# A hybrid decoder block on one core: where the state-space tables are made, and when their rest runs

## The chip, the core and the metric

The kernel runs on one of the eight cores of a Trainium2 chip. Time is device time of one execution in microseconds (us), from the start of the program to its end. The kernel before has a median of 2892.49 us in three runs (2890.32 to 2893.48). Its profiled execution, from which all rows come, took 2894.66 us, with a span of 2892.9 us from the first to the last instruction.

A core has five engines with a queue of instructions each: TensorE (PE, matmuls; its weight loads are listed as PEld), VectorE (DVE), ScalarE (ACT), GpSimd (POOL) and SyncE (SP). Each works through its own queue in order; they wait for each other by semaphores. Here SP issues the loads of weights, and nearly all other transfers are issued by POOL, in the order in which they stand in its queue. A transfer whose issue waits holds up all that stand behind it in that queue.

## The reference

One decoder block on 512 tokens with 16 learned meta tokens ahead (528 rows, width 2048), all in float32. Attention with low-rank queries and keys (MLA) and a diagonal complex state-space layer (S5) run in parallel on the same normalised input:

```python
n = rms_norm(h, norm_mix)
q_lat, kv_lat, k_r, u, gates = split(n @ w_in)          # widths 512, 512, 64, 1024, 4096
q, kv = rms_norm(q_lat) @ w_q_up, rms_norm(kv_lat) @ w_kv_up
attn_out = softmax(causal(q k^T)) v @ w_attn_proj       # 16 heads, rope on 64 dims
y = gelu(s5_scan(u, ...))                               # 64 groups of 16 inputs, 64 states
ssm_out = (y @ w_glu_val) * sigmoid(y @ w_glu_gate)
h += (sigmoid(g0) * attn_out + sigmoid(g1) * ssm_out) @ w_out
h += (silu(m @ w_ffn_gate) * (m @ w_ffn_up)) @ w_ffn_down   # m = rms_norm(h)
out = rms_norm(h)[:, 16:]
```

The scan is x_t = a x_(t-1) + B u_t with y_t = Re(C x_t) + D u_t, where a, B and C follow from parameters by exponentials, sines and complex products. What depends on the parameters alone is called tables here.

## The kernel before

**Matmuls.** A float32 weight tile is split into a high part (`whi`, a rounded copy made by ACT) and a rest (`wlo`, a subtraction on DVE); so is each moving operand. A product is the sum of three matmuls. `dense` (L389) makes a tile of 128 output columns from weight blocks of 128 x 1024: eight slices by three products, 24 matmuls of 512 columns, or 48 of 264 where all 528 rows are made. Such a run over one weight block is called a block below. `Weights.use` (L280) splits the block that comes two later (`AHEAD`), so a split stands in the queues of ACT and DVE between the work of neighbouring blocks.

**Work beside the blocks.** After each block `bg()` (L363) runs first the calls in `later` that are due, then each generator given to `beside`, up to an allowance: a `yield` names the cost of what was just issued in units of about a microsecond, and the generator goes on while its account is positive. So the order of instructions is that in which this code is written out.

**First stage (0 to 305 us).** Tiles j = 0 to 7 of `u` over 16 blocks; `rstd` of the input comes in tile 2, and `evac_u` (L864) empties the first three tiles then. After these, four tiles of the query latent (8 blocks), four of the key latent (8 blocks) and one of the rope key (2 blocks). `ssm_first` (L730) runs beside them from tile 1 on with an allowance of 4.0: `ssm_params` (L518), then for each of four groups of states `ssm_tables` (L665: the rotation table `ER`, an expansion in two halves into `ssA`, its products on PE into `psQ`, and its transposes on PE into `psB`, kept as `bd`) and, for the first three groups, `ssm_powers` (L717: another expansion, kept as `cd`). `normed` (L891) turns the key latent into operands in four pieces (rows `ev<-H`, `H<-ev` on DVE). `run_out()` (L929) issues what is left of the generator behind the last block, and only then come the load of the rope table `in_kcs`, the rotation of the rope key, and the attention's first products (`up_rope`).

**Attention (305 to 584 us).** Heads are pipelined by hand; the change does not touch it.

**Attention projection (584 to 850 us).** 16 tiles of two blocks each, 32 blocks, `ev` buffers for the results and stores to `ao`. Beside them run `ssm_main` (L737, one step per block) and `x_products` (L1353), which loads x in eight pairs, scales them on DVE and stores them with three combinations to `xd`, operands of the gates. `ssm_main` first loads `U`, `ER` and the output tables, makes the power table of the last group, and loads `ssA` from `bd`. Then each group takes five steps: `states` of the first half (PE, from `ssA` and `U`) with `rotate` (DVE) and the second `outputs` of the group before; `states` of the second half, then the loads of `ssA` and `U` for the next group, the stores of results (`yd`) and the loads of the output tables (`ssB` from `kd`, eight transfers, and two of `cd`); `scan`; `back`, and the load of `ER` for the next group, which has a single buffer; and the first `outputs`. From tile 12 on the gates' operands are loaded and split (L1374).

**After 850 us** follow the gates, the gated unit, the output projection and the feed-forward layer. The change does not touch them.

Of the kernel before, what the change touches and what calls it, by code (L numbers as in the profile page):

```python
# [297 lines left out]
def _emit(nc, sp, pp, dp, A, out):  # L298
# [45 lines left out]
    ed = dp.tile([4, P, 4 * BP * NC_], F32, name="ed")  # L344
# [3 lines left out]
    c3 = dp.tile([P, 2 * BP * 48], F32, name="c3")  # L348
# [316 lines left out]
    def ssm_tables(b):  # L665
# [14 lines left out]
        ER = sb([P, 4, BP, NC_], F32, "ER")  # L680
        for i in range(2):
            ACT.activation(ER[:, 2 * i, :, :18], tabs["rt"][i][:, js], AF.Copy)
        POOL.memset(ER[:, 3, :, 0], 0.0)
        DVE.tensor_copy(ER[:, 3, :, 1:], e8[:, 2, js].unsqueeze(2).to_broadcast([P, BP, NC_ - 1]))
        yield 0.7
        for m, k in ((17, 17), (34, 31)):
            double((ER[:, 0], ER[:, 2]), m, k, BP, T1, T2)
            yield 1.0 + 0.05 * k
        ts(ER[:, 1], ER[:, 2], -1.0, None, MUL)
        POOL.dma_start(ed[b], ER.rearrange("p a j c -> p (a j c)"))  # L690
        yield 0.5
# [22 lines left out]
        if b == 3:  # L714
            POOL.dma_start(c3, C48.rearrange("p a j q -> p (a j q)"))

# [13 lines left out]
    def ssm_first():  # L730
        yield from ssm_params()
        for b in range(4):
            yield from ssm_tables(b)
            if b < 3:
                yield from ssm_powers(b)

    def ssm_main():  # L737
# [16 lines left out]
        def load_e(b):  # L754
            ER = sb([P, 4, BP * NC_], F32, "ER")
            POOL.dma_start(ER.rearrange("p a n -> p (a n)"), ed[b])
            nxt_["E", b] = ER

# [66 lines left out]

        load_u(0)
        load_e(0)
        load_t(0)
        C48 = sb([P, 2, BP, 48], F32, "sC")
        POOL.dma_start(C48.rearrange("p a j q -> p (a j q)"), c3)  # L830
        tabs["C48"] = C48
        yield 1
        for _ in ssm_powers(3):
            yield 1
        load_b(0)
        nxt_["m"] = [sb([P, 2, T], F32, t) for t in ("T1", "T2", "v", "w")]
        for b in range(4):
            states(b, 0)
            rotate(b, 0)
            if b:  # L840
                outputs(b - 1, 1)
            yield 1
            states(b, 1)
            rotate(b, 1)
            if b < 3:
                load_b(b + 1)
                load_u(b + 1)
            if b:
                store(b - 1)
                load_t(b)  # L850
            yield 1
            scan(b)
            yield 1
            back(b)
            if b < 3:
                load_e(b + 1)
            yield 1
            outputs(b, 0)
            yield 1
        outputs(3, 1)  # L860
# [15 lines left out]
    for j in range(8):  # L876
        if j == 2:
            d2 = ps([P, 2, 512], "D")
            o = [(d2[:, 0, :HT], 0, HT), (d2[:, 1, :HT], HT, T)]
        else:  # L880
            o = halves("A", "B")
        dense(n, KT, o)
        pend.append((j, o))
        if j >= 2:
            while pend:
                evac_u(*pend.pop(0))
        if j == 1:
            beside(ssm_first(), 4.0)
# [464 lines left out]
    def x_products():  # L1353
# [6 lines left out]

        load(0)
        yield 2
        for i in range(8):
            if i < 7:
                load(i + 1)
            for m in range(2):
# [7 lines left out]
    begin = {12: [L("XD", *range(4)), L("XA", *range(4))],  # L1374
             13: [S("XD", *range(4)), L("XA", *range(4, 8)), L("B12", 2)],
             14: [S("XA", *range(4)), L("B12", 3, 0, 1)],
             15: [S("XA", *range(4, 8)), S("B12", *range(4)), L("T12", *range(8))]}
    beside(ssm_main(), 1.0)
    beside(x_products(), 2.2)
    for j in range(KT):  # L1380
        p = ps([P, 512], "A")
        dense(at, KT, [(p, 0, SEQ)])
        t = ev(SEQ)
# [3 lines left out]
        for h in begin.get(j, ()):  # L1387
            h()
# [422 lines left out]
```

## Time and profile before

| | |
|---|---|
| median of 3 runs | 2892.49 us |
| profiled execution | 2894.66 us (span 2892.9 us) |
| PE busy | 2759.4 us, 95% of the span |
| DVE busy | 2049.5 us, 71% |
| ACT busy | 1217.5 us, 42% |
| POOL busy | 478.7 us, 17% |
| PE's share of the chain that ended last | 86% |
| mean granted clock of PE | 0.976 |

The page sums up the whole span, and most of it is one full stage after another; what a change in one stage is worth is read from that stage. So the rows further down are from stretches: how long PE was busy in one, at what granted clock (1.00 is 2.4 GHz, 0.5 is 1.2 GHz), and what it waited for. The time before an instruction in which its engine did nothing stands in brackets at the end of its row, with the engine, tile or transfer that ended it.

### The profile page before, as it was taken

How to read it: one execution, taken by the hardware profiler on the slowest of the kernel's cores; microseconds unless marked ns; L12 is line 12 of the kernel's file. 1: busy time of each engine (PE TensorE's matmuls, PEld its weight loads, DVE VectorE, ACT ScalarE, POOL GpSimd, SP SyncE). 2: the span in 40 equal slices, each digit the busy share in tenths (PEclk: the TensorE clock that was granted, in tenths of full speed). 3: DMA queues.
4: the chain of work that ended last, by engine and by line, in shares of the span. 5: the costliest groups of instructions: out<-in, count | busy, mean ns of one | idle time of the engine just before them, and what ended most of it. 6: DMA issues, size and time to landing. Idle time of an engine off the chain costs nothing.

```text
span 2892.9 us, 50212 instructions
## 1 busy us (share of the span) xinstructions
PE 2759.4 (95%) x20782; PEld 2603.3 (90%) x20782; DVE 2049.5 (71%) x2690; ACT 1217.5 (42%) x1766; POOL 478.7 (17%) x731
## 2 busy tenths in 40 slices
PE   8995999968899999999999999999999999999997
PEld 7984899946779999888889999999999999999997
DVE  7775666655437777543368888888888888878896
ACT  4232555522235444432234444444444445353445
POOL 2032211134430000111213000000000003030102
PEclk9996999989999999999999999999999999999999
DMA  4453222268673443544443333433434336474542
GB/s 169 140 166 117 79 65 66 61 202 282 191 262 128 154 146 132 167 138 146 142 138 115 139 132 132 146 129 123 144 125 139 136 128 248 163 269 153 198 166 96
DMA packets 126788, 431.49 MB, mean 149 GB/s; under 512 B 18240, under 2 KB 23040, under 8 KB 124448
## 3 DMA queue, kind: packets, MB, share of 16 engines
q1 hardware_dynamic: 76672, 263.36, 26.8%
q0 software_dynamic: 49104, 163.82, 17.2%
q8 instruction: 163, 2.67, 0.4%
q10 hardware_dynamic: 784, 1.11, 0.1%
q14 instruction: 65, 0.53, 0.1%
HBM read 344.87 MB, written 77.66 MB: 146 GB/s over the span
## 4 chain that ended last, share of the span: by engine, by line
PE 86%; DVE 6%; DMA 3%; issue 2%; ACT 1%; POOL 1%; DVEq 0%; SPq 0%; ACTq 0%; POOLq 0%
PE psA L316 50%; PE psB L316 22%; PE psQ L316 6%; PE psV L316 5%; PE psD L316 2%; DVE wlo L263 1%; DVE T L323 1%; DVE ev L323 1%; DVE S L323 1%; DMA H<-in_xT 1%; DMA ssA<-bd 0%; PE psB L710 0%; POOL ssB L766 0%; PE psA L1123 0%; ACT whi L262 0%
## 5 line engine op out<-in xcount | busy, mean ns | idle before, releaser
L316 PE MATMUL psA<-S,whi 128*128 128x256 f32 (+2 forms) x5136 | 1124.3, 309 | 20.8 <-DVE ev L323 6.7
L316 PEld LDWEIGHTS psA<-S,whi 128*128 128x128 f32 x5136 | 845.4, 190 | 76.5 <-issue 10.2
L316 PE MATMUL psA<-S,wlo 128*128 128x256 f32 (+2 forms) x2568 | 791.5, 308 | 7.9 <-DVE wlo L263 7.9
L263 DVE TENSOR_TENSOR wlo<-raw,whi 128x1024 fp32r<-128x1024 f32 (+1 forms) x479 | 590.6, 1234 | 190.2 <-ACT whi L262 188.3
L262 ACT ACTIVATE whi<-raw 128x1024 fp32r<-128x1024 f32 (+1 forms) x479 | 504.4, 1055 | 458.1 <-PE psA L316 213.4
L316 PEld LDWEIGHTS psA<-S,wlo 128*128 128x128 f32 x2568 | 485.8, 189 | 34.0 <-DVE wlo L263 8.3
L263 DVE TENSOR_TENSOR wlo<-cmb,whi 128x1024 fp32r<-128x1024 f32 x225 | 274.8, 1221 | 96.4 <-ACT whi L262 95.3
L316 PE MATMUL psB<-S,whi 128*128 128x256 f32 (+1 forms) x1632 | 330.3, 284 | 0.5 <-ACT ssB L711 0.5
L262 ACT ACTIVATE whi<-cmb 128x1024 fp32r<-128x1024 f32 x225 | 237.7, 1056 | 201.5 <-DVE wlo L263 121.6
L316 PEld LDWEIGHTS psB<-S,whi 128*128 128x128 f32 x1632 | 266.2, 190 | 1.3 <-ACT ssB L711 1.0
L316 PE MATMUL psB<-S,wlo 128*128 128x256 f32 (+1 forms) x816 | 230.8, 283 | 0.0
L316 PEld LDWEIGHTS psB<-S,wlo 128*128 128x128 f32 x816 | 154.7, 190 | 0.0
L1331 POOL DMA_DIRECT2D td<-sC x22 | 15.8, 718 | 764.6 <-ACT ev L1250 718.3
L316 PE MATMUL psA<-H,whi 128*128 128x512 f32 (+2 forms) x448 | 120.4, 355 | 8.9 <-DVE ev L323 8.0
L316 PEld LDWEIGHTS psA<-H,whi 128*128 128x128 f32 x448 | 78.2, 192 | 19.9 <-DVE ev L323 8.2
L243 DVE TENSOR_TENSOR cmb<-raw,raw 128x1024 f32<-128x1024 f32 x75 | 91.3, 1218 | 6.3 <-DMA raw<-in_wst 5.2
L323 DVE TENSOR_TENSOR H<-H,psA 128x256 f32<-128x256 f32 (+1 forms) x42 | 22.5, 535 | 97.2 <-POOL H L323 88.2
L243 DVE TENSOR_TENSOR cmb<-cmb,raw 128x1024 f32<-128x1024 f32 x75 | 91.3, 1218 | 0.0
L243 DVE TENSOR_TENSOR raw<-raw,raw 128x1024 f32<-128x1024 f32 x75 | 91.3, 1218 | 0.0
L243 DVE TENSOR_TENSOR cmb<-raw,cmb 128x1024 f32<-128x1024 f32 x75 | 91.3, 1217 | 0.0
L1250 ACT ACTIVATE ev<-psA 128x256 f32<-128x256 f32 x114 | 43.4, 381 | 100.7 <-PE psA L316 100.7
L316 PE MATMUL psA<-H,wlo 128*128 128x512 f32 (+2 forms) x224 | 78.0, 348 | 0.0
(678 smaller groups left out, 5463.4 us busy)
## 6 DMA issues: line engine op xcount, KB each, us to landing
raw<-in_wst SPq DMA_DIRECT2D x485, 512.0 KB, 3.6
td<-sC POOLq DMA_DIRECT2D x22, 512.0 KB, 3.2
td<-H POOLq DMA_DIRECT2D x40, 256.0 KB, 3.3
S<-td POOLq DMA_DIRECT2D x40, 256.0 KB, 6.8
H<-sg POOLq DMA_DIRECT2D x16, 512.0 KB, 4.0
ed<-ER POOLq DMA_DIRECT2D x4, 1056.0 KB, 5.1
ER<-ed POOLq DMA_DIRECT2D x4, 1056.0 KB, 7.8
bd<-ssB POOLq DMA_DIRECT2D x4, 1024.0 KB, 5.2
```

Source lines behind the costliest of these rows:

```text
L243: self.nc.vector.tensor_tensor(t, g(a), g(b), op=op)
L262: self.nc.scalar.activation(hi[:, a:b], w[:, a:b], AF.Copy)
L263: self.nc.vector.tensor_tensor(lo[:, a:b], w[:, a:b], hi[:, a:b], op=ALU.subtract)
L316: PE.matmul(o, lhsT=l, rhs=r, start=start, stop=stop, skip_group_check=more)
L323: eng.tensor_tensor(o, a, b, op=op)
L1250: ACT.activation(snap[name], o, AF.Copy)
L1331: POOL.dma_start(dst[0:2].rearrange("f p n -> p f n"), pair)
```

## The change

Four things change. `ssm_first` makes the power tables of all four groups, starts after tile 2 with an allowance of 5.0, and leaves two of the four parts of `ER` (a sign change and a decay) to be made in the projection, on ACT (`more_e`). `ssm_main` has new steps: loads first, `states` two blocks later, tables and results behind `scan`, `U` of the next group behind `back`, both `outputs` of a group in the two steps of the next. `x_products` begins its loads two and its products three blocks later. The results of the projection go through one buffer (`sC`) in place of three, and the operands of the gates are loaded and split in blocks 26 to 32, in another order.

```diff
-    ed = dp.tile([4, P, 4 * BP * NC_], F32, name="ed")
+    ed = dp.tile([4, P, 2, BP * NC_], F32, name="ed")
...
-        ER = sb([P, 4, BP, NC_], F32, "ER")
+        ER = sb([P, 2, BP, NC_], F32, "ER")
         for i in range(2):
-            ACT.activation(ER[:, 2 * i, :, :18], tabs["rt"][i][:, js], AF.Copy)
-        POOL.memset(ER[:, 3, :, 0], 0.0)
-        DVE.tensor_copy(ER[:, 3, :, 1:], e8[:, 2, js].unsqueeze(2).to_broadcast([P, BP, NC_ - 1]))
-        yield 0.7
+            ACT.activation(ER[:, i, :, :18], tabs["rt"][i][:, js], AF.Copy)
+        yield 0.3
...
-        ts(ER[:, 1], ER[:, 2], -1.0, None, MUL)
...
             yield from ssm_tables(b)
-            if b < 3:
-                yield from ssm_powers(b)
+            yield from ssm_powers(b)
...
-            POOL.dma_start(ER.rearrange("p a n -> p (a n)"), ed[b])
+            POOL.dma_start(ER[:, 0::2], ed[b])
             nxt_["E", b] = ER
+
+        def more_e(b):
+
+            js, ER = slice(b * BP, (b + 1) * BP), nxt_["E", b]
+            d = ER[:, 3].rearrange("p (j c) -> p j c", c=NC_)
+            POOL.memset(d[:, :, 0], 0.0)
+            ACT.activation(d[:, :, 1:], e8[:, 2, js].unsqueeze(2).to_broadcast([P, BP, NC_ - 1]), AF.Copy)
+            ACT.activation(ER[:, 1], ER[:, 2], AF.Copy, scale=-1.0)
...
+        load_b(0)
         load_u(0)
         load_e(0)
-        load_t(0)
-        C48 = sb([P, 2, BP, 48], F32, "sC")
-        POOL.dma_start(C48.rearrange("p a j q -> p (a j q)"), c3)
-        tabs["C48"] = C48
+        nxt_["m"] = [sb([P, 2, T], F32, t) for t in ("T1", "T2", "v", "w")]
         yield 1
-        for _ in ssm_powers(3):
-            yield 1
-        load_b(0)
-        nxt_["m"] = [sb([P, 2, T], F32, t) for t in ("T1", "T2", "v", "w")]
+        yield 1
+        more_e(0)
         for b in range(4):
+            if b:
+                outputs(b - 1, 0)
             states(b, 0)
             rotate(b, 0)
+            yield 1
             if b:
                 outputs(b - 1, 1)
-            yield 1
             states(b, 1)
             rotate(b, 1)
             if b < 3:
                 load_b(b + 1)
-                load_u(b + 1)
+            yield 1
+            scan(b)
             if b:
                 store(b - 1)
-                load_t(b)
-            yield 1
-            scan(b)
+            load_t(b)
             yield 1
             back(b)
             if b < 3:
                 load_e(b + 1)
+                load_u(b + 1)
             yield 1
-            outputs(b, 0)
+            if b < 3:
+                more_e(b + 1)
             yield 1
+        outputs(3, 0)
+        yield 1
         outputs(3, 1)
         store(3)
...
-        if j == 1:
-            beside(ssm_first(), 4.0)
+        if j == 2:
+            beside(ssm_first(), 5.0)
...
+        yield 2.2
+        yield 2.2
         load(0)
-        yield 2
+        yield 2.2
+        load(1)
+        yield 2.2
         for i in range(8):
-            if i < 7:
+            if 0 < i < 7:
                 load(i + 1)
...
-    begin = {12: [L("XD", *range(4)), L("XA", *range(4))],
-             13: [S("XD", *range(4)), L("XA", *range(4, 8)), L("B12", 2)],
-             14: [S("XA", *range(4)), L("B12", 3, 0, 1)],
-             15: [S("XA", *range(4, 8)), S("B12", *range(4)), L("T12", *range(8))]}
+
+    begin = {26: [L("XD", *range(4)), L("B12", 2, 3)], 27: [L("B12", 0, 1), L("XA", *range(4))],
+             28: [S("XD", *range(4)), S("B12", 2)], 29: [S("B12", 3), L("XA", *range(4, 8))], 30: [S("B12", 0, 1)],
+             31: [S("XA", *range(4))], 32: [L("T12", *range(8)), S("XA", *range(4, 8))]}
+    for i, fs in begin.items():
+        later.extend([i, f] for f in fs)
...
-        t = ev(SEQ)
+        t = sb([P, SEQ], F32, "sC")
         ACT.activation(t, p, AF.Copy)
         POOL.dma_start(ao[j], t)
```

Where this puts instructions is seen in the built programs. First DVE at the end of the first stage. In the kernel before the four latent pieces are over when these rows begin: the end of the fourth `ER`, the two halves of its expansion (`T`, `ssA`), `sK` from the products on PE, then the eviction of the rope key (`S<-psA`, `S<-psB`) and its product with the rope table.

```order
L323 TENSOR_TENSOR ER_2562<-T_183_2557,T_184_2558 128x8x31
L330 TENSOR_SCALAR ER_2562<-ER_2562 128x528
L323 TENSOR_TENSOR T_183_2557<-sw_2553,spw_185 128x1024
L323 TENSOR_TENSOR T_184_2558<-sw_2553,spw_185 128x1024
L323 TENSOR_TENSOR ssA_2581<-T_183_2557,T_184_2558 128x1024
L323 TENSOR_TENSOR T_183_2557<-sw_2553,spw_185 128x1024
L323 TENSOR_TENSOR T_184_2558<-sw_2553,spw_185 128x1024
L323 TENSOR_TENSOR ssA_2581<-T_183_2557,T_184_2558 128x1024
L323 TENSOR_TENSOR sK_2555<-psQ_2588,sK_2555 128x256
L323 TENSOR_TENSOR S_193_2657<-psA_2404,rstd_114 128x264
L323 TENSOR_TENSOR S_193_2657<-psB_2405,rstd_114 128x264
L323 TENSOR_TENSOR S_193_2657<-S_193_2657 128x528
```

In the changed kernel, at the same place, the second half of the fourth power table (`ssA`), a weight split, the four latent pieces (`ev<-H`, `H<-ev`) and the eviction:

```order
L323 TENSOR_TENSOR ssA_2497<-T_178_2495,T_179_2496 128x1024
L263 TENSOR_TENSOR wlo_2579<-raw_2320,whi_2578 128x1024
L326 SCALAR_TENSOR_TENSOR ev_2632<-H_138_1945,gv_78,KS_1792 128x528
L320 TENSOR_TENSOR H_189_2634<-ev_2632,H_189_2634 128x528
L326 SCALAR_TENSOR_TENSOR ev_2637<-H_154_2146,gv_78,KS_1792 128x528
L320 TENSOR_TENSOR H_191_2639<-ev_2637,H_191_2639 128x528
L326 SCALAR_TENSOR_TENSOR ev_2642<-H_168_2308,gv_78,KS_1792 128x528
L320 TENSOR_TENSOR H_193_2644<-ev_2642,H_193_2644 128x528
L326 SCALAR_TENSOR_TENSOR ev_2647<-H_181_2501,gv_78,KS_1792 128x528
L320 TENSOR_TENSOR H_195_2649<-ev_2647,H_195_2649 128x528
L323 TENSOR_TENSOR S_196_2656<-psA_2507,rstd_113 128x264
L323 TENSOR_TENSOR S_196_2656<-psB_2508,rstd_113 128x264
```

The fourth table now stands far ahead of the pieces, the fourth power table right ahead of them, and the eviction and the rope product follow the pieces at once.

Second, POOL's queue at the beginning of the projection, in the kernel before, from the first stores of `x_products` on (`in_xT`, `xd`: x and its products; `ao`: results of the projection; `cd<-ssA`: the fourth power table; `ssA<-bd`: the operand of the first `states`):

```order
L1331 DMA xd<-H_528_6183 128x2x512
L1339 DMA xd<-H_530_6189 128x512
L1340 DMA xd<-H_530_6189 128x512
L1385 DMA ao<-ev_6233 128x512
L1359 DMA H_536_6270<-in_xT 128x2x512
L1331 DMA xd<-H_529_6185 128x2x512
L1339 DMA xd<-H_537_6274 128x512
L1340 DMA xd<-H_537_6274 128x512
L727 DMA cd<-ssA_6229 64x1024 x4
L751 DMA ssA_6316<-bd 128x2048
```

In the changed kernel the projection begins with:

```order
L743 DMA ssA_6155<-bd 128x2048
L737 DMA U_6157<-ud 16x16x66 x8
L748 DMA ER_6166<-ed 128x2x528
L1392 DMA ao<-sC_6202 128x512
L755 MEMSET ER_6166 128x8
L1360 DMA H_535_6259<-in_xT 128x2x512
L743 DMA ssA_6311<-bd 128x2048
L1360 DMA H_538_6313<-in_xT 128x2x512
L1392 DMA ao<-sC_6315 128x512
L763 MEMSET ssB_6351 128x2048
```

The first `ssA<-bd` moved from behind the second group of `xd` stores and the `cd` stores to the head, and the loads of x moved behind it.

Third, POOL's queue in the second group of states, where the load of `U` for the third stands. In the kernel before, `U` follows `ssA<-bd`, and results (`yd`) and tables (clear of `ssB`, loads from `kd`) follow `U`:

```order
L751 DMA ssA_6734<-bd 128x2048
L745 DMA U_6736<-ud 16x16x66 x8
L823 DMA yd<-H_560_6582 16x16x64 x8
L763 MEMSET ssB_6753 128x2048
L766 DMA ssB_6753<-kd 16x16x16
L766 DMA ssB_6753<-kd 16x16x32
```

In the changed kernel the end of the tables (the last load from `kd`, two from `cd`), a pair of x, its products, a result of the projection and `ER` come ahead of `U`:

```order
L766 DMA ssB_6712<-kd 16x2048
L770 DMA H_565_6722<-cd 128x1024
L770 DMA H_566_6723<-cd 128x1024
L1360 DMA H_567_6726<-in_xT 128x2x512
L1332 DMA xd<-H_562_6660 128x2x512
L1340 DMA xd<-H_568_6730 128x512
L1341 DMA xd<-H_568_6730 128x512
L1392 DMA ao<-sC_6738 128x512
L748 DMA ER_6780<-ed 128x2x528
L737 DMA U_6782<-ud 16x16x66 x8
```

The tables changed places with `U`: what was behind it in the queue is now ahead of it, `yd` and the other loads from `kd` too.

## Rows read from the trace of the kernel before

**Rows 1.** Stretches: length, busy us (instructions) by engine, PEclk, DMA share, GB/s:

```profile
114.40:244.70 130.30, 122.23 (x919) 109.91 (x917) 97.00 (x134) 37.83 (x59) 34.56 (x55) 0.95 0.46 148
...
244.70:276.25 31.55, 7.51 (x81) 6.66 (x81) 21.24 (x34) 5.89 (x12) 7.12 (x14) 0.54 0.28 87
...
584.00:850.40 266.40, 216.30 (x1539) 175.10 (x1539) 125.02 (x160) 67.77 (x97) 109.08 (x182) 0.90 0.73 230
```

**Rows 2.** Timeline of PE, first stage: start, us, instruction, count, [idle before <-released by]:

```profile
53.53 0.56 PE L316 MATMUL psA<-S,whi 128*128 128x264 f32 x1 [6.70 <-DVE ev L323]
...
177.99 0.66 PE L710 MATMUL psB<-ident,ssA 128*128 128x128 f32 x4 [0.69 <-ACT ssB L711]
...
264.97 0.43 PE L316 MATMUL psQ<-U,ssA 128*64 128x32 f32 x4 [20.23 <-DVE ssA L323]
...
268.53 3.42 PE L316 MATMUL psQ<-U,ssA 128*64 128x32 f32 x60 [3.13 <-DVE ssA L323]
...
292.22 0.59 PE L316 MATMUL psA<-H,whi 128*128 128x264 f32 x1 [7.98 <-DVE ev L323]
```

**Rows 3.** Waits of PE from 584 to 851: total us, times, longest:

```profile
PE psD L316 <- DMA ssA<-bd: 18.0, 1, 18.0
PE psV L316 <- DMA ssB<-kd: 17.0, 2, 8.9
PE psA L316 <- DVE wlo L263: 7.9, 1, 7.9
PE psA L316 <- ACT acc L1271: 4.0, 1, 4.0
```

**Rows 4.** Chain that ended last, in the projection: start, us, matmuls:

```profile
672.46 1.08 PE psD L316 x32
...
799.28 2.02 PE psQ L316 x64
...
801.30 44.80 PE psA L316 x192
```

**Rows 5.** Timeline of DVE, first stage: a split, half an expansion, last piece, rope:

```profile
131.30 1.23 DVE L263 TENSOR_TENSOR wlo<-raw,whi 128x1024 fp32r<-128x1024 f32 x1 [1.65 <-ACT whi L262]
...
132.44 2.35 DVE L323 TENSOR_TENSOR T<-sw,spw 128x1024 f32<-128x1024 f32 x2
...
134.83 1.23 DVE L323 TENSOR_TENSOR ssA<-T,T 128x1024 f32<-128x1024 f32 x1
...
255.26 0.71 DVE L320 TENSOR_TENSOR H<-ev,H 128x528 fp32r<-128x528 f32 x1 [0.77 <-ACT H L319]
...
255.88 0.42 DVE L684 COPY ER<-se 128x520 f32<-128x520 f32 x1
...
284.13 0.71 DVE L323 TENSOR_TENSOR S<-S 128x528 f32<-128x528 f32 x1 [11.03 <-DMA S<-in_kcs]
```

**Rows 6.** Timeline of POOL, projection: issues of one group:

```profile
574.93 4.61 POOL L745 DMA_DIRECT2D U<-ud  x8 [21.58 <-PE psD L316]
...
768.66 4.49 POOL L823 DMA_DIRECT2D yd<-H  x8 [7.82 <-ACT H L818]
...
773.14 1.82 POOL L763 MEMSET ssB<- 128x2048 f32 x1
...
775.26 4.38 POOL L766 DMA_DIRECT2D ssB<-kd  x8 [0.29 <-POOL ssB L763]
...
779.63 1.10 POOL L770 DMA_DIRECT2D H<-cd  x2
...
780.73 0.55 POOL L1385 DMA_DIRECT2D ao<-ev  x1
```

**Rows 7.** Transfers in the projection: KB and median to landing; landing of `ud`:

```profile
U<-ud POOLq DMA_DIRECT2D x8, 66.0 KB, 6.9
...
DMA to landing us min/median/max: 2.9/6.2/10.3
```

**Rows 8.** Waits of DVE from 584 to 851: total us, times, longest:

```profile
DVE H L326 <- DMA H<-in_xT: 32.1, 3, 17.2
```

More of the change, by code (lines that the diff above doesn't have):

```diff
@@ L343, in _emit @@
     bd = dp.tile([4, P, BP * 2 * P], F32, name="bd")
-    ed = dp.tile([4, P, 4 * BP * NC_], F32, name="ed")
+    ed = dp.tile([4, P, 2, BP * NC_], F32, name="ed")
     cd = dp.tile([4, 2, P, BP * P], F32, name="cd")
     xd = dp.tile([8, 4, P, SEQ], F32, name="xd")
-    c3 = dp.tile([P, 2 * BP * 48], F32, name="c3")
     ao = dp.tile([KT, P, SEQ], F32, name="ao")
@@ L678, in ssm_tables @@
             ACT.activation(C48[ph, :, :, c:c + 16], C[ph, :, js], AF.Copy)
-        ER = sb([P, 4, BP, NC_], F32, "ER")
+        ER = sb([P, 2, BP, NC_], F32, "ER")
         for i in range(2):
-            ACT.activation(ER[:, 2 * i, :, :18], tabs["rt"][i][:, js], AF.Copy)
-        POOL.memset(ER[:, 3, :, 0], 0.0)
-        DVE.tensor_copy(ER[:, 3, :, 1:], e8[:, 2, js].unsqueeze(2).to_broadcast([P, BP, NC_ - 1]))
-        yield 0.7
+            ACT.activation(ER[:, i, :, :18], tabs["rt"][i][:, js], AF.Copy)
+        yield 0.3
         for m, k in ((17, 17), (34, 31)):
-            double((ER[:, 0], ER[:, 2]), m, k, BP, T1, T2)
+            double((ER[:, 0], ER[:, 1]), m, k, BP, T1, T2)
             yield 1.0 + 0.05 * k
-        ts(ER[:, 1], ER[:, 2], -1.0, None, MUL)
-        POOL.dma_start(ed[b], ER.rearrange("p a j c -> p (a j c)"))
-        yield 0.5
+        POOL.dma_start(ed[b], ER.rearrange("p a j c -> p a (j c)"))
         BL = sb([P, 2, BP, CL * 16], F32, "ssA")
@@ L713, in ssm_tables @@
         POOL.dma_start(bd[b], BT.rearrange("p j a c -> p (j a c)"))
-        if b == 3:
-            POOL.dma_start(c3, C48.rearrange("p a j q -> p (a j q)"))
     def ssm_powers(b):
@@ L1386, in _emit @@
         assert j < 12 or not bg_gens
-        for h in begin.get(j, ()):
-            h()
     st.free |= {"H0", "H1", "H2", "H3", "H4", "H5", "H6"}
```

## The prediction, made before the changed kernel ran

> **What bounds the kernel now.** First the page: TensorE (PE) is busy for 95% of the span and makes up 86% of the chain that ended last, so time can come only from stretches in which PE stands still or runs at its lower clock level. Second, the slices of the span on the page: PE stands at 8 or 9 tenths in all but the two regions below. Third, the table by stretches [rows 1]. The attention, and all that follows the projection, is full on the page, and the change does not touch it. From 244.7 to 276.3 us PE is busy for 7.5 of 31.6 us at 0.54, and from 584.0 to 850.4 us for 216.3 of 266.4 us at 0.90. Those two stretches are what the change works on.
>
> The first one: the run-up to the attention. PE's waits [rows 2] show 6.70 us at 53.53 (it waits for VectorE to empty a PSUM bank), then 20.23 and 3.13 us at 264.97 and 268.53 (it waits for `ssA`, the last state-space table on VectorE), then 7.98 us at 292.22 (VectorE had not read a bank, because it waited for the cosine table).
>
> The second: the attention projection with the rest of the state-space layer. PE's waits there [rows 3] are 18.0 us for the load of `ssA` from `bd`, 17.0 us in two pieces for `ssB` from `kd`, 7.9 us for a weight split and 4.0 us for operands of the gates. What the work itself needs comes from the undisturbed pieces of the chain [rows 4]: 192 matmuls, eight blocks, in 44.80 us, so 5.60 us a block; 1.08 us for one `states` call and 2.02 us for one `outputs` call. The 32 blocks, eight `states` and eight `outputs` make 179.2 + 8.6 + 16.2 = 204.0 us. The stretch took 266.4, so 62.4 us are waits (50.1 us not busy) or work done at the lower clock level (the rest, 12.3 us).
>
> **The change, part by part: first stage.** VectorE (DVE) ended the last latent piece at 255.26 + 0.71 = 255.97 us; only then came the fourth table, up to the matmuls at 268.53 [rows 5, 2]: 12.6 us. The fourth power table, which stood in the projection, is two halves of 2.35 + 1.23 us [rows 5], 7.2 us. Both now stand before that last piece. The copy of the decay and the sign change go to ScalarE: four times two operations like the copy of 0.42 us [rows 5], 3.4 us less. DVE therefore has 16.4 us more before its last piece. Against that, the parameters start one column tile later, behind the evictions: the 6.70 us wait at 53.53 goes, since the first evictions no longer stand behind the two exponentials, and all but 0.1 us of it moves the blocks forward, 6.6 us.
>
> When is the last piece done now? DVE was busy for 97.0 of the 130.3 us up to 244.7 [rows 1], so 33.3 us were idle. If the new work sank into those gaps, the piece would end 6.6 us earlier, at 249; if none did and nothing moved forward, at 255.97 + 16.4 = 272.4. The gaps are largely tied to something: per column tile 1.65 us in which the split waits for ScalarE [rows 5], eight times, and per power table some 4.5 us in which `ssA` cannot be written, since PE transposes it (a batch of four takes 0.66 us and waits 0.69 us for the copy [rows 2]). Five units a block plus a split of 1.2 us is also more than the 5.6 us of a block. So I let none sink in and keep only the earlier start: 265.8.
>
> What follows the last piece had 36.3 us to the restart at 292.22: the fourth table, its matmuls, and then a key-rope table that was waited for until 284.13 because its load stood in the POOL queue behind all of that. In the new order this load comes right behind the power table and has the 8.4 us of the four pieces to land. What remains is the 0.84 us eviction and the step from 284.13 to 292.22, which is not changed (the product, the copy, the load of the cosine table behind it in the queue): 8.9 us. PE restarts at 265.8 + 8.9 = 274.7 instead of 292.2: **17 us saved**; by the two ends 258 and 281, so 34 or 11.
>
> **Second stage.** Blocks are counted from the start of the projection. The loads of `ssA` now go out in block 1 and `states` runs at the end of block 3, some 14 us later, and no power table stands between: the 18.0 us go. Tables and outputs: the loads from `kd` are issued one block after both `states` calls, without eight loads of `U` ahead of them, and used three blocks later: the 17.0 us go where POOL has room. The 7.9 us go: the loads of x precede their use by two blocks. The 4.0 us go: the operands that the gates read first are split in blocks 28 to 30. The evacuation moved to a single buffer (`sC`) waits for the store of the tile before it, 11 us earlier; ScalarE may then stand for several microseconds, but weights are split two blocks ahead, which covers up to 11 us.
>
> What is late next is the load of `U` for the next group. It now stands behind the tables in the POOL queue. From the release of `ssA` in the second group, the queue issues: `ssA` 0.6, an x load 0.7, three stores of products (ready 6.2 us after the release), eight `yd` stores 4.5, clear and gap 2.1, eight `kd` loads 4.4, two `cd` loads 1.1, x load and three stores 2.6, store of the projection and `ER` 1.1, eight `U` loads 4.6: 26.6 us (the large ones in [rows 6]; single issues take 0.55 us or a little more). The last `U` lands 6.9 us later [rows 7], at 33.5. PE wants it after four blocks and one `outputs`: 22.4 + 2.0 = 24.4. That is a new wait of 9.1 us, and a restart at the lower clock level, about 3 us (12.3 us were lost over four or five restarts). In the third group no x load stands ahead: 20.2 + 6.9 against 24.4, 2.7 us; in the first, 18.5 + 6.9, 1.0 us. The last has no next `U`. Sum: 16 us. The stage then costs 204.0 + 16 = 220 us instead of 266.4: **46 us saved**. With every transfer hidden it is 62; with each of the three `U` loads at the longest landing of 10.3 us (3.4 us more) and each restart at 3 us, about 31.
>
> What these transfers cost is also where a rule can be held against a row. Loads of `U`, 66 KB each, took a median of 6.9 us here [rows 7]. The Trainium skill, "DMA: Bandwidth & Descriptors", section "Anatomy of one DMA — SWDGE (gpsimd) path", puts a transfer from this queue at some 2.0 us plus its bytes over 436 GB/s; an estimate by that page is 2.2 us for `U`. By it only the second group would wait, 4.4 us plus the restart, and the kernel would take about 2822 us. The trace disagrees by a factor of three, in a stretch whose DMA engines are busy 0.73 of the time [rows 1], so I keep the row.
>
> Elsewhere nothing moves. The profiled execution took 2894.66 us, span 2892.9; the sum is 2894.7 - 17 - 46 = 2831.7. The median of the runs lies 2.2 us below the profiled one: **2830 us**.
>
> **Rivals.** (A) Everything is hidden: the table work sinks into DVE's gaps and the `U` loads arrive in time. For it: 33 idle us on DVE, POOL busy for only 109 of 266 us. Against: the tied gaps and the queue sum above. 2894.7 - 34 - 62 = 2799, on the median 2796. (B) DVE becomes the bound of the first stage: evictions and splits come late, PE waits before the matmuls of the third and fourth table and the clock falls again, so that these last longer and hold `ssA` longer. If four tables add 5 us each and the idle time stays, the last piece ends at 292 and PE restarts at 301, 9 us later than now: 2894.7 + 9 - 46 = 2858, on the median 2855. (C) Slower: the loads of x hold DVE. Three of them held it for 32.1 us before, one for 17.2 us [rows 8]; DVE's next weight split stands behind the wait. They now stand behind the loads of tables, `ER` and `U`. Were all eight held for 17.2 us, each would exceed the 11.2 us that the splits are ahead by 6 us and add a restart of 3 us: 72 us against 63 saved, 2904, on the median 2901. It decides from a hold of about 16 us on each; from the queue I get some 8 us for the third load and less for the others. (D) No change: the order of instructions shows that the moves are there, so this needs new waits of just the size of the gains.
>
> **Chances.** My sum 0.60 (its own range 2812 to 2850), A 0.20, B 0.12, C 0.04, D 0.04. A measurement of this kernel tells no difference under 0.2%, 5.8 us. So faster 0.92, same 0.04, slower 0.04. The range for eight in ten reaches into A and past B: 2798 to 2862.
>
> **What would show it.** Right: no wait of PE for `ssA` from `bd`, for `ssB` from `kd`, nor of 20 us for a table on DVE; the last latent piece at about 266 us and PE's restart at about 275; a wait of PE in `states` of the third group for `U` of 5 to 10 us, clock down behind it; the first matmul of the gates some 220 us after the projection's first. Wrong: PE waits for `wlo` in the projection (C), waits for `ssA` before the attention that sum to over 15 us (B), or no wait for `U` at all (A).

## The result, and the profile after

The changed kernel has a median of 2854.49 us in four runs (2851.15 to 2856.01), the kernel before 2891.40 us on the same chip. The ratio is 0.9871, with a 95% interval of 0.9854 to 0.9888: 37 us faster. I had forecast 2830 us and a range of 2798 to 2862. The profiled execution took 2853.81 us, with a span of 2852.0.

The waits of PE in the projection (total us, times, longest), in answer to [rows 3]:

```profile
PE psD L316 <- DMA U<-ud: 8.9, 1, 8.9
PE psD L316 <- DMA ao<-sC: 8.1, 1, 8.1
PE psV L316 <- DMA ssB<-kd: 3.9, 1, 3.9
PE psD L316 <- DMA H<-ud: 3.6, 1, 3.6
PE psV L316 <- issue: 1.9, 1, 1.9
```

The wait of 18.0 us for `ssA` is gone, and so are those for `wlo` and for the gates' operands. New are 20.7 us in `states` (psD), which wait for `U` (the tile has the tags `U` and `H0` in turn, so it also reads `H<-ud`). One of them is put down to `ao<-sC`, a store that was issued right behind the last load of `U`; `states` reads nothing of `ao`, so I count this wait to `U`. Of the 17.0 us for `kd`, 3.9 are still there; 1.9 more stand right behind, in products that read a `cd` load, and the profile names no transfer for them. The stretch, from the projection's first matmul to the first gates matmul on `acc`, in answer to the last row of [rows 1]:

```profile
573.60:814.07 240.47, 213.73 (x1539) 174.14 (x1540) 119.59 (x156) 72.04 (x104) 114.11 (x191) 0.94 0.80 245
```

It is 240.5 us instead of 266.3: 25.9 saved, where I had 46. The timeline of PE, in answer to [rows 2]:

```profile
197.91 3.42 PE L316 MATMUL psQ<-U,ssA 128*64 128x32 f32 x60 [7.98 <-DVE ssA L323]
...
237.25 3.21 PE L316 MATMUL psQ<-U,ssA 128*64 128x32 f32 x60 [4.45 <-DVE ssA L323]
...
281.36 0.81 PE L316 MATMUL psA<-H,whi 128*128 128x264 f32 x2 [4.82 <-DVE ev L323]
...
573.60 0.50 PE L316 MATMUL psA<-S,whi 128*128 128x512 f32 x1 [1.20 <-ACT S L319]
...
681.13 2.03 PE L316 MATMUL psD<-U,ssA 128*64 128x66 f32 x32 [8.91 <-DMA U<-ud]
```

PE restarts at 281.36 instead of 292.22, and the projection begins 10.5 us earlier (573.60 for 584.06), where I had 17. The wait of 20.2 us is gone; in its place stand waits for tables inside the blocks. At 681.13 the 32 matmuls take 2.03 us instead of 1.08: the lower clock level behind a wait. The remaining 4.6 us of the span's 40.9 lie behind the stretch, where I had put nothing; 2.6 of them are in the first block of the gates (8.1 us before, behind its wait, 5.5 now).

### The profile page after: what moved, and what is told of

It is laid out like the page before. It is cut to its first block, busy times and chain, and to the rows that moved or that the text cites. A ratio compares the mean times of both kernels' runs of the same rounds, so it can differ in the third digit from the quotient of the medians.

```text
span 2852.0 us, 50236 instructions
## 1 busy us (share of the span) xinstructions
PE 2756.4 (97%) x20782; PEld 2601.1 (91%) x20782; DVE 2047.4 (72%) x2682; ACT 1222.1 (43%) x1774; POOL 479.1 (17%) x729
## 4 chain that ended last, share of the span: by engine, by line
PE 84%; DVE 6%; DMA 4%; issue 3%; POOL 1%; ACT 1%; DVEq 0%; POOLq 0%; ACTq 0%
PE psA L316 48%; PE psB L316 22%; PE psQ L316 6%; PE psV L316 5%; PE psD L316 2%; DVE T L323 1%; DMA ER<-ed 1%; DVE wlo L263 1%; DVE S L323 1%; DVE ev L323 1%; DMA xd<-H 1%; DMA sw<-in_sb 0%; ACT whi L262 0%; PE psA L1124 0%; PE psB L705 0%
## 5 line engine op out<-in xcount | busy, mean ns | idle before, releaser
L263 DVE TENSOR_TENSOR wlo<-raw,whi 128x1024 fp32r<-128x1024 f32 (+1 forms) x479 | 591.5, 1236 | 193.8 <-ACT whi L262 191.9
L262 ACT ACTIVATE whi<-cmb 128x1024 fp32r<-128x1024 f32 x225 | 237.7, 1056 | 202.5 <-DVE wlo L263 142.0
L316 PEld LDWEIGHTS psA<-H,whi 128*128 128x128 f32 x448 | 78.5, 194 | 22.3 <-issue 6.6
```

Source lines behind the costliest of these rows:

```text
L262: self.nc.scalar.activation(hi[:, a:b], w[:, a:b], AF.Copy)
L263: self.nc.vector.tensor_tensor(lo[:, a:b], w[:, a:b], hi[:, a:b], op=ALU.subtract)
L316: PE.matmul(o, lhsT=l, rhs=r, start=start, stop=stop, skip_group_check=more)
```

## What the experiments settled

**Where the stretch's gain went.** First a look at the POOL queue of the changed kernel, at the loads of `U` for the third group:

```profile
661.56 1.12 POOL L770 DMA_DIRECT2D H<-cd  x2
662.67 0.73 POOL L1360 DMA_DIRECT2D H<-in_xT  x1
663.40 0.74 POOL L1332 DMA_DIRECT2D xd<-H  x1
664.43 0.58 POOL L1340 DMA_DIRECT2D xd<-H  x1 [0.29 <-issue]
665.00 0.56 POOL L1341 DMA_DIRECT2D xd<-H  x1
665.72 0.54 POOL L1392 DMA_DIRECT2D ao<-sC  x1 [0.17 <-issue]
666.72 0.72 POOL L748 DMA_DIRECT2D ER<-ed  x1 [0.46 <-issue]
668.95 0.60 POOL L737 DMA_DIRECT2D U<-ud  x1 [1.51 <-DMA H<-cd]
670.63 0.58 POOL L737 DMA_DIRECT2D U<-ud  x1 [1.09 <-DMA H<-cd]
672.21 0.56 POOL L737 DMA_DIRECT2D U<-ud  x1 [1.00 <-DMA H<-in_xT]
673.49 1.80 POOL L737 DMA_DIRECT2D U<-ud  x3 [0.71 <-DMA xd<-H]
675.45 0.56 POOL L737 DMA_DIRECT2D U<-ud  x1 [0.16 <-issue]
677.83 0.56 POOL L737 DMA_DIRECT2D U<-ud  x1 [1.82 <-DMA ER<-ed]
```

The eight loads took 9.4 us, not the 4.6 of [rows 6]. Five of the six `U` rows show a wait for a transfer, and it is always the one that was issued eight places earlier: it has to have landed. The first `U` load waits for the first `cd` load, the third for the load of x, the eighth for `ER`, which took 10.8 us. The built program says so too; in its POOL queue each transfer waits for one of eight completion slots, in turn (here, in the loads for the fourth group, `ER` holds slot 5 and the last `U` load waits for it):

```
307 L748 DMA ER_7129<-ed 128x2x528 [waits DMASW5_49,DVE_49]
308 L737 DMA H_594_7131<-ud 16x16x66 [waits DMASW6_49]
309 L737 DMA H_594_7131<-ud 16x16x66 [waits DMASW7_49]
310 L737 DMA H_594_7131<-ud 16x16x66 [waits DMASW0_49]
...
315 L737 DMA H_594_7131<-ud 16x16x66 [waits DMASW5_49]
```

In the kernel before, the loads of `U` in [rows 6] came when the queue had stood idle for 21.6 us, so the slots were free. That row is from the first group; the other rows under the same heading are from the last. The wait was there to be seen in the loads for the second group, where the last one waits for `ssA`, eight places ahead:

```profile
646.47 3.94 POOL L745 DMA_DIRECT2D H<-ud  x7
655.02 0.56 POOL L745 DMA_DIRECT2D H<-ud  x1 [4.61 <-DMA ssA<-bd]
```

The second, third and fourth group's loads took 9.1, 9.0 and 6.4 us in that kernel; the prediction's sum was made from the first.

What the runs had to tell apart: is it the slots (theory L), or the order and the slots of the queue together (Q), or the order alone (O), or are the DMA engines, 0.80 busy, simply full (B)? These letters, and D and P further down, are those of the expectations, not of the prediction's rivals. The table has for each run the projection's first matmul, the stretch as above, PE's waits for `U` and for `kd` in it, the median, and the ratio to the kernel before on the same chip. `U` includes waits in `states` that the profile puts down to the transfer issued right behind `U`; `kd` includes those put down to nothing behind it. Runs on the first stage are in it as well. In six profiles with the same first stage the first matmul came at 573.0 to 574.8 us, and in six with the same projection the stretch was 238.9 to 245.4 us, so smaller differences are not read.

| run | first matmul | stretch | `U` | `kd` | median | ratio |
|---|---|---|---|---|---|---|
| changed kernel | 573.6 | 240.5 | 20.7 | 5.8 | 2854.5 | 0.9871 (0.9854 to 0.9888) |
| u_first | 574.2 | 239.2 | 15.9 | 5.3 | 2857.5 | 0.9877 (0.9860 to 0.9894) |
| er_sp | 574.7 | 240.0 | 18.1 | 7.6 | 2854.4 | 0.9868 (0.9853 to 0.9883) |
| x_slow | 573.5 | 241.7 | 19.0 | 7.1 | 2854.5 | 0.9871 (0.9856 to 0.9885) |
| u_sp | 574.8 | 233.2 | 4.7 | 17.9 | 2848.7 | 0.9852 (0.9838 to 0.9867) |
| uy_sp | 573.0 | 237.9 | 21.7 | 0 | 2848.3 | 0.9839 (0.9818 to 0.9860) |
| no_x (leaves work out) | 610.8 | 224.2 | 12.9 | 0 | | |
| best | 567.0 | 216.7 | 0 | 0 | 2826.2 | 0.9759 (0.9742 to 0.9776) |
| pw_own | 569.3 | 240.1 | | | 2851.2 | 0.9857 (0.9842 to 0.9872) |
| pw_first | 577.1 | 242.8 | | | 2859.5 | 0.9883 (0.9868 to 0.9898) |
| pool_half | 591.5 | 245.4 | | | 2872.9 | 0.9933 (0.9916 to 0.9949) |
| pool_pw | 589.3 | 238.9 | | | 2873.1 | 0.9933 (0.9918 to 0.9948) |
| less_dve (leaves work out) | 560.3 | 243.2 | 22.3 | 6.6 | 2844.5 | 0.9829 (0.9809 to 0.9849) |

**u_first**, `U` ahead of `ER`:

```diff
-                load_e(b + 1)
                 load_u(b + 1)
+                load_e(b + 1)
```

> The load of U for the next group is issued ahead of the load of ER, nothing else is changed. Theory L (completion lanes): each transfer of the POOL queue waits for the transfer eight issues earlier to have landed; in the changed kernel the eighth issue before the last U load is the load of ER, which takes 10.6 to 11.9 us, so U is late by that. With ER behind U, the three waits of PE for U (3.65, 8.91 and 8.11 us, 20.7 in all) fall to under 6 us together, and the kernel takes 12 to 24 us less: 2830 to 2842. Theory B (bandwidth): U lands late because the DMA engines are 0.7 to 0.8 busy and all transfers are slow; the order of two neighbours changes little: 2850 to 2858, the waits sum to over 15 us. A cost under either: ER lands later, ScalarE stands longer for it (16.4 us at most now), which could turn into a wait of PE for a weight split.

Measured: no gain. The last load of `U` went out only 3 us earlier (674.79 for 677.83), since it now waited for the slots of `cd`, x and the products. A new wait of 3.1 us came in `states` of the second group: VectorE was late with the rotation ahead of it, after 4.6 us for a load of x and 3.7 us for a store of products. So `ER` is not the cause by itself.

**er_sp**, the load of `ER` on SyncE's queue:

```diff
-            POOL.dma_start(ER[:, 0::2], ed[b])
+            (nc.sync if b else POOL).dma_start(ER[:, 0::2], ed[b])
```

> The load of ER for the second to fourth group goes out on SyncE's queue, at the same place in the program; bytes and order are the same otherwise. Theory L: the last U load's lane is then that of an attention store, landed sooner; PE's waits for U fall from 20.7 to 5 to 12 us and the kernel to 2836 to 2846. Theory B: the same bytes are moved, so the waits stay over 15 us and the time at 2850 to 2858.

Measured: no gain, for the same reason: the last load of `U` for the third group went out only 2 us earlier (675.87). Up to here B had the better of it.

**x_slow**, allowance 1.5 instead of 2.2 for the products of x:

```diff
-    beside(x_products(), 2.2)
+    beside(x_products(), 1.5)
```

> The products of x are spread over about 23 blocks instead of 16 (allowance 1.5 a block instead of 2.2): the same transfers, 12.6 MB of the 54 in the stretch, but fewer of them beside the loads of the second and third group, more beside those of the last, which has no U load behind it. Theory B: where the engines are less crowded, U and kd land earlier; the waits (26.5 us in the changed kernel) fall to 8 to 18, the stretch to 226 to 235, kernel 2838 to 2848. Theory L, since a product's stores hold slots of the queue too, expects the same sign. A third (O): the wait is set by the order of the queue alone, so it stays within 3 us: kernel 2850 to 2857.

Measured: no gain, against both L and B; O alone had expected this. From 573.6 to 640 the DMA share fell from 0.84 to 0.74, and the wait for `U` that ends in this window stayed (3.3 us for 3.65).

**u_sp**, the loads of `U` on SyncE's queue:

```diff
-                POOL.dma_start(U[i * 16:(i + 1) * 16],
+                (nc.sync if b else POOL).dma_start(U[i * 16:(i + 1) * 16],
```

> The eight loads of U for the second to fourth group go out on SyncE's queue, between the weight loads, at the same place in the program. Moving ER or swapping the two loads left the waits of PE for U, kd at 18 to 24 us (changed kernel 26.5 with all), which speaks against the lanes of the POOL queue as the only cause. Theory L: the POOL queue has eight slots fewer to wait for, U is issued at once: waits for U under 6 us, first gates matmul of acc at 218 to 226 us after the projection's first matmul (240.5 in the changed kernel), kernel 2834 to 2842. Theory B (the DMA engines are the bound, 0.79 to 0.82 busy in this stretch): U lands at the same time whatever its queue; the stretch 236 to 242 us, kernel 2849 to 2857.

Measured: `U` as L has it, the stretch between the two. Waits of PE in the projection:

```profile
PE psV L316 <- DMA ssB<-kd: 14.0, 2, 8.3
PE psV L316 <- issue: 3.9, 2, 2.0
PE psD L316 <- DMA H<-ud: 3.0, 1, 3.0
PE psD L316 <- DMA U<-ud: 1.7, 1, 1.7
```

`U` is nearly in time (4.7 us for 20.7), with the same bytes and with the DMA engines 0.96 busy from 640 to 700 us. PE runs ahead into the next late transfer, the `kd` tables, whose loads stand in the POOL queue behind the `yd` stores and their slots.

**uy_sp**, the `yd` stores on SyncE's queue as well:

```diff
-                POOL.dma_start(yd[g0 * 16:(g0 + BG) * 16, t].rearrange(
+                nc.sync.dma_start(yd[g0 * 16:(g0 + BG) * 16, t].rearrange(
```

> As the run with U on SyncE's queue (2848.7; waits for U fell from 20.7 to 4.7 us, but those for kd rose from 5.8 to 17.9), and the eight stores of outputs (yd) of each group on SyncE's queue too. Theory Q (order and slots of the POOL queue): the kd loads stand right behind the yd stores and come 5 to 8 us earlier without them; the waits for kd fall under 6 us and the stretch to 220 to 226 us (233.2 with U alone, 240.5 in the changed kernel); kernel 2834 to 2843. Theory B (DMA engines, 0.96 busy from 640 to 700): the same bytes, so kd is late anyhow: stretch 231 to 236, kernel 2846 to 2853. A danger: weights queue behind the stores on SyncE's queue, and PE waits for splits.

Measured: the waits for `kd` are gone, as Q has it, and `U` is late again (10.3 of its 21.7 us are put down to the load of weights right behind it). On SyncE's queue it now stands behind the `yd` stores (first load for the third group at 667.9 us, 654.4 with `U` alone), and SyncE waits for slots too. Its own waits in this stretch:

```profile
SPq L737 <- DMA H<-v: 21.9, 4, 9.4
...
SPq L737 <- DMA raw<-in_wst: 4.0, 1, 4.0
```

`H<-v` is a transfer of the rotation `back`, issued on ScalarE's queue. In the built program the transfers of both queues take the same eight slots in turn, so `U`, written behind `back`, waits for what `back` sends.

**no_x**, the projection without the products of x; copies of x fill `xd` before the attention:

```diff
+    for i in range(8):
+        for h in range(2):
+            POOL.dma_start(xd[i, 2 * h:2 * h + 2], A["xT"][i::8][:, :, META:])
...
-    beside(x_products(), 2.2)
```

> The changed kernel without the products of x in the projection: their loads and stores (12.6 MB of 54, 32 issues of the POOL queue) and their VectorE work are left out; the gates read copies of x made before the attention instead, so the output is another, and only the stretch of the projection is compared. Theories B and Q both expect the waits for U and kd (26.5 us) to fall, since bytes and slots both go: under 6 us, stretch 206 to 216. If they stay over 15 us, the groups' own transfers are in each other's way, and x has no part in it: stretch 228 or more.

Measured: in between. With 12.6 MB fewer and a DMA share of 0.72 PE still waits 12.9 us for `U`. In the POOL queue the last load of `U` waits for `ER` in the second and in the fourth group:

```profile
647.09 0.73 POOL L748 DMA_DIRECT2D ER<-ed  x1
647.82 2.83 POOL L737 DMA_DIRECT2D H<-ud  x5
...
656.98 0.56 POOL L737 DMA_DIRECT2D H<-ud  x1 [2.35 <-DMA ER<-ed]
...
741.16 0.56 POOL L737 DMA_DIRECT2D H<-ud  x1 [2.82 <-DMA ER<-ed]
```

Here the slot rule stands by itself: the load of `ER` is eight places ahead, and the last `U` goes out when it has landed, 9 to 10 us after its issue.

**best**: `U` and `yd` on SyncE's queue, `U` issued two blocks earlier (ahead of `yd` and of `back`), and the buffers of pw_own below:

```diff
                 load_b(b + 1)
+                load_u(b + 1)
             yield 1
...
                 load_e(b + 1)
-                load_u(b + 1)
```

> U (second to fourth group) and the yd stores on SyncE's queue as in the run before, but U's loads issued two blocks earlier, right behind the load of the next ssA, ahead of the yd stores; and the power expansions of the first three tables in tiles of their own (569.3 for the projection's first matmul). In the run before, the kd loads were in time (no wait) and only U was late (21.7 us), since on SyncE's queue it stood behind the yd stores, and its turn behind transfers of the rotation that wait for VectorE. Theory Q (order and slots of the queues): waits for U and kd together under 8 us, stretch 210 to 220 us, first matmul of the projection at 568 to 571, kernel 2820 to 2832. Theory B (the DMA engines have no more to give; U is late wherever it stands): waits over 15 us, stretch 230 to 238, kernel 2838 to 2848.

Measured: 2826.15 us in five runs, faster than both kernels; its interval lies clear of the changed kernel's. PE's waits in the projection, and its stretch:

```profile
PE psA L316 <- DVE wlo L263: 3.8, 1, 3.8
PE psV L316 <- DMA H<-v: 3.6, 2, 2.8
```

```profile
567.00:783.71 216.71, 208.87 (x1540) 169.78 (x1540) 119.67 (x156) 72.26 (x104) 82.59 (x135) 0.98 0.90 273
```

No wait for `U` or `kd`, in a stretch (from the projection's own start, so without the gain of pw_own's buffers ahead of it) that is 24 us shorter with the same bytes, and with a DMA share of 0.90. The 24 loads of `U` on SyncE's queue even took longer to land (a median of 8.6 us, 4.4 to 13.8, for 5.7) and were in time all the same. So B is refuted as the cause: the engines had more to give. What made `U` and `kd` late is when their issues got their turn, by the order of the queues and their slots; how much each of these two does by itself no run separates. One move alone only hands the wait on. That the new wait of 3.8 us for a split comes from weights behind the other transfers on SyncE's queue is likely, but was not tried by itself.

**Where the first stage's gain went.** VectorE reads the PSUM bank of each tile, so its reads show how far the blocks are. Three of them in the kernel before: the eighth tile of `u`, and the second and fourth tile of the query latent behind it (the tenth and twelfth tile in all):

```profile
114.40 0.65 DVE L323 TENSOR_TENSOR ev<-psA,rstd 128x264 f32<-128x264 f32 x1
...
137.11 0.68 DVE L323 TENSOR_TENSOR H<-psA,rstd 128x512 f32<-128x512 f32 x1
...
167.39 0.68 DVE L323 TENSOR_TENSOR H<-psA,rstd 128x512 f32<-128x512 f32 x1
```

And in the changed kernel, with its last latent piece:

```profile
107.16 0.65 DVE L323 TENSOR_TENSOR ev<-psA,rstd 128x264 f32<-128x264 f32 x1
...
133.82 0.68 DVE L323 TENSOR_TENSOR H<-psA,rstd 128x512 f32<-128x512 f32 x1
...
170.15 0.68 DVE L323 TENSOR_TENSOR H<-psA,rstd 128x512 f32<-128x512 f32 x1
...
272.36 0.71 DVE L320 TENSOR_TENSOR H<-ev,H 128x528 fp32r<-128x528 f32 x1 [0.77 <-ACT H L319]
```

The lead of 7.2 us is there at the eighth tile; it is 3.3 at the tenth, and at the twelfth the blocks are 2.8 us behind. Theory P: VectorE and PE hand `ssA` to and fro. From 60 to 276 us PE waits for tables, and VectorE for PE's transposes:

```profile
PE psQ L316 <- DVE ssA L323: 16.5, 5, 8.0
DVE ssA L323 <- PE psB L705: 13.0, 3, 5.5
```

Theory D: VectorE's own work sets the pace.

**pw_own** (powers of three groups in two free tiles, `H6` and `H7`; the rest as it was):

```diff
...
-        CLt = sb([P, 2, BP, P], F32, "ssA")
+        CLt = sb([P, 2, BP, P], F32, "ssA") if b == 3 else [sb([P, 2 * T], F32, t)[:, :BP * P].rearrange("p (j m) -> p j m", m=P) for t in ("H6", "H7")]
...
```

> The power expansions of the first three tables are written to two free tiles instead of ssA; order of instructions as in the changed kernel. Theory P (one buffer handed to and fro): VectorE's 13.0 us of waits for PE's transposes, and the 16.5 us that PE waits for tables, come from ssA being shared by table and powers. Without it the last latent piece ends at about 266 us instead of 273.07 and the first matmul of the attention projection comes at 565 to 568 instead of 573.6; kernel 2846 to 2849. Theory D (VectorE is full): the pieces come in the order written, and only VectorE's work sets the time: first matmul at 572 to 575, kernel 2852 to 2857.

Measured: VectorE's waits for the transposes fell from 13.0 to 3.8 us, PE's for tables from 16.5 to 12.3, and the projection began 4.3 us earlier. P is part of it, though the projection was expected at 565 to 568 and came at 569.3. The total alone could not tell (the intervals overlap).

**pw_first** (all powers in tiles of their own, and issued ahead of the PE work of their table):

```diff
         yield from expand(BL, Bt, js, 0, 1, T1, T2)
-        yield 1
+        yield from ssm_powers(b)
...
             yield from ssm_tables(b)
-            yield from ssm_powers(b)
```

> Powers in tiles of their own for all four tables, and expanded ahead of the PE work of their table, so that PE asks for a table one and a half blocks after VectorE was given it. Theory P: PE's waits for ssA inside the first stage (16.5 us) fall under 5, the clock stays up, the first matmul of the projection comes at 560 to 565, kernel 2841 to 2847. Theory D: PE's waits go, but the last latent piece still ends at 270 or later, as VectorE has the same work: first matmul at 570 or later, kernel 2850 to 2857.

Measured: later by 3.5 us, against P and within what D has. PE's waits for `ssA` are gone, and others have come in their place (0 to 330 us):

```profile
PE psA L316 <- ACT whi L262: 16.4, 4, 7.3
PE psB L705 <- ACT ssB L706: 11.1, 10, 3.8
PE psQ L316 <- POOL KS L323: 5.5, 1, 5.5
```

**pool_half** and **pool_pw** (one product of each half on GpSimd; the second with the buffers of pw_own):

```diff
+        tt(a2, sv(1), pws(1), MUL, POOL)
...
-        tt(a2, sv(1), pws(1), MUL)
...
+        tt(a2, sv(0), pws(1), MUL, POOL)
...
-        tt(a2, sv(0), pws(1), MUL)
...
```

> In each half of an expansion (tables and powers) one of the two products is made by GpSimd, issued a step ahead, so that VectorE does 16 instructions of 1.2 us less in the first stage. Theory D (VectorE is the bound there): the last latent piece comes 8 to 15 us earlier (258 to 265 instead of 273.07), first matmul of the projection 560 to 566, kernel 2840 to 2847. Theory P (ssA handed to and fro between VectorE and PE): PE's wait for tables shrinks only by the shorter expansions, 2 to 5 us: first matmul 568 to 572. A GpSimd product of this size is not in the trace; its 128x528 product takes 1.3 us, so 2.6 for 1024 columns; should VectorE and GpSimd slow each other, VectorE's 1.2 us grow and nothing is won.

> The same with the power expansions of the first three tables in tiles of their own (as in the run that had 569.3 for the projection's first matmul). Theory D and theory P together: gains add, first matmul at 556 to 563, kernel 2836 to 2844. If only one of the two holds, it equals the better of the two single kernels within 2 us.

Measured: both worse by 18 us than the changed kernel, where either theory had expected a gain. GpSimd took 2.1 to 2.5 us a product, and VectorE stood for it; its splits also became longer, 1.54 us in place of 1.29. The waits of VectorE (60 to 276 us) in pool_half:

```profile
DVE ssA L323 <- POOL T L323: 36.4, 8, 10.6
```

The Trainium skill ("GPSIMD Engine Reference", section "1. Specifications") has the SBUF interfaces of the two shared, with contention where a VectorE instruction has two SBUF inputs; the longer splits agree. This run moved work and did not test D.

**less_dve** does: three instructions of 1.2 us in the second half of each power expansion left out (a ScalarE copy fills the tile):

```diff
-        tt(a1, sv(1), pws(0), MUL)
-        tt(a2, sv(0), pws(1), MUL)
-        tt(d4(1), a1, a2, op_im)
+        if sign < 0:
+            ACT.activation(d4(1), d4(0), AF.Copy)
+        else:
+            tt(a1, sv(1), pws(0), MUL)
+            tt(a2, sv(0), pws(1), MUL)
+            tt(d4(1), a1, a2, op_im)
```

> The second half of each power expansion, three VectorE instructions of 1.2 us, is replaced by one ScalarE copy of the first half (the powers' imaginary part is left out): 14.4 us less on VectorE in the first stage, nothing else. Theory D (VectorE's work sets the end of the first stage, almost 1:1): first matmul of the projection at 558 to 564 instead of 573.6, kernel 2837 to 2846. Theory P (waits of VectorE and PE for one another around ssA): 565 to 570, kernel 2846 to 2851. If neither, under 3 us: 571 or later.

Measured: 14.4 us less work on VectorE, and the projection begins 13.3 us earlier. That is D, almost one to one. The stretch behind it stayed as it was (243.2, within the spread above).

The same is read from VectorE's busy time, from the end of `rstd`, ahead of all this work, to the end of the last latent piece (the third of the busy times behind the length): the kernel before, the changed kernel, and less_dve:

```profile
44.89:255.97 211.08, 185.08 (x1415) 172.34 (x1413) 154.06 (x308) 51.91 (x76) 43.11 (x74) 0.92 0.42 138
```

```profile
44.44:273.07 228.63, 200.77 (x1519) 184.46 (x1517) 170.19 (x327) 55.74 (x88) 51.14 (x86) 0.91 0.43 134
```

```profile
44.50:259.91 215.41, 198.89 (x1519) 182.88 (x1517) 156.36 (x316) 59.78 (x92) 51.05 (x86) 0.93 0.46 142
```

VectorE is busy for 154.1, 170.2 and 156.4 us and idle for 57.0, 58.4 and 59.1: what is added or left out goes into the length one to one, and the idle time stays. Of the runs looked at in this way only pw_own makes some of it go (53.6 us).

## Why the prediction came out as it did

Direction and range held; the gain was 37 us where I had 62, and both stages fell short by about the same share.

- **First stage, -17; measured -10.5.** What follows the last piece was right: 8.3 us to the restart for 8.9. The failing step is "I let none sink in and keep only the earlier start: 265.8". Its first half held: VectorE had 16.1 us more to do, for the 16.4 of the sum, and none of it went into idle time. Its second half did not: the lead of 6.6 us was no credit on top of that. The wait that went was PE's; to bring the last piece forward, the lead would have had to come out of VectorE's idle time, and that was 57.0 us before and 58.4 now. The blocks' lead was spent by the twelfth tile, and the piece ended at 273.1, near my upper end of 272.4.
- **Second stage, -46; measured -25.9.** The 18.0, 7.9 and 4.0 us went, as said. The failing term is the queue sum, 26.6 us for the third group's `U`, made of issues that had found their slots free. The table has the three groups that wait for a `U`: us from the release of `ssA` to the end of the last `U` issue, from there to PE's start, from the release to PE's being ready, and PE's wait; forecast first, then measured.

| `U` for group | queue | landing | PE ready | wait |
|---|---|---|---|---|
| second | 18.5, 24.5 | 6.9, 3.4 | 24.4, 24.2 | 1.0, 3.65 |
| third | 26.6, 38.2 | 6.9, 2.7 | 24.4, 32.0 | 9.1, 8.91 |
| fourth | 20.2, 29.9 | 6.9, 2.4 | 24.4, 24.2 | 2.7, 8.11 |

The queue was 6.0, 11.6 and 9.7 us longer; in the trace its waits for a transfer eight places ahead sum to 7.7, 8.5 and 7.6 us there. That the third group's wait came out as forecast is luck: the queue was too short in the sum by 11.6 us, the landing too long by 4.2, and PE itself came 7.6 us later, since the `kd` tables were late too (5.8 us). For the other two groups I had counted no restart at the lower clock level either. "The 17.0 us go where POOL has room" was the same error; 5.8 stayed.
- **The clock.** 240.5 less 204.0 of work and 26.5 of waits leaves 10.0 us at the lower level, for 12.3 before; I had 3, for one restart.
- **The rule on transfers.** By the Trainium skill ("DMA: Bandwidth & Descriptors", section "Anatomy of one DMA — SWDGE (gpsimd) path") an estimate for `U` is 2.2 us. In the changed kernel the median over all 32 loads was 5.7 (2.6 to 11.2), nearer to the row of 6.9. But PE waits for the last load of a group, and those three landed in 3.5, 2.8 and 2.6 us, nearer to that estimate. Either way it mattered less than the waits ahead of the issue.
- **Signs.** Those of being right that came: no wait for `ssA` from `bd`, none of 20 us for a table (the longest was 8.0), and 8.9 us for `U` in the third group with the clock down behind it. The last piece at 266, the restart at 275, the stretch of 220 us and the end of the waits for `kd` did not come: 273.1, 281.4, 240.5 and 3.9.
- **Rivals.** B's time (2855) is what was measured, and its sign, waits for `ssA` over 15 us, was there (16.5). That VectorE bounds the first stage is what less_dve shows. The time is luck all the same: B has the restart 9 us later and the projection 46 us shorter, and measured were 10.5 us earlier and 25.9 us shorter. Of A's 62 us in the projection the last run has 50 (216.7 for 266.3), so they were to be had, but in another order of the queues. C did not come: PE had no wait for `wlo`; x held VectorE for 16.2 us in two waits, 32.1 before [rows 8]. The single `sC` buffer cost PE nothing.

## What to carry to other kernels

The duration of an issue that found its slot free is not its price behind a busy queue; read the same issue at every place where the trace has it. Count the transfers ahead of it: with eight slots taken in turn, one slow transfer holds up the eighth issue behind it, and a burst of eight goes no faster than the eight before it land. When one engine's work sets the pace of a stage, starting the others earlier buys nothing, and time in which that engine is idle need not take up new work; and where a wait only moves from one transfer to the next, move all that stand in that queue before judging the idea.

## What the runs showed that I had not expected

Half of `ER` (528 KB, strided) landed in a median of 10.7 us over the four groups, where the whole of it (1056 KB) had taken 7.8. Transfers issued on SyncE's and ScalarE's queues share their slots in this program: SyncE stood for 21.9 us behind ScalarE's in uy_sp. And a DMA share of 0.80 was no sign of a full system: the last kernel moved 273 GB/s in its stretch, for 245, at a share of 0.90.
